# A diffusion block on one core: the order of the first stage (context, conditioning, context keys and values, latent transposes)

## The chip, the cores and the metric

The kernel runs on one core of a Trainium2 chip. The metric is the device time of one execution in microseconds (us), as the median of several runs. The engines of the core are TensorE (PE, matmuls; PEld its weight loads), VectorE (DVE), ScalarE (ACT), GpSimd (POOL) and SyncE (SP, which issues most DMAs). Each engine works through its own list of instructions strictly in the order of that list; an instruction that waits holds back everything behind it on that engine.

## The reference, cut to what matters

```
mod   = split(silu(c)     @ w_ada + b_ada, 6)        # latents: sh1, sc1, g1, sh2, sc2, g2
mod_c = split(silu(c_ctx) @ w_ada + b_ada, 6)        # context: sh1c, sc1c, ...
h_lat = rmsnorm(x,   norm1_g) * (1 + sc1)  + sh1     # 1024 tokens x 1024
h_ctx = rmsnorm(ctx, norm1_g) * (1 + sc1c) + sh1c    #  256 tokens x 1024
# of the context only the keys, the values and the two gate inputs are needed:
k_c, v_c, af_c, ab_c = h_ctx @ w_in[:, ...]          # 512, 1024, 16, 16 columns
q, k, v, r, u, v', af, ab, ga, gb = h_lat @ w_in     # all of them
# two gated linear attention scans (forward, backward) that start from the context's
# state, a gated MLP over chunks, their merge, a residual, a SwiGLU block, a final rmsnorm
```

All is float32. A product is made of three passes over operands that are split into a high part (rounded to the matmul's format) and a low part (the remainder): high x high, high x low, low x high.

## The kernel before, in words

Everything stands in one function, `block_kernel`. The Python code states operations; a scheduler then gives each engine its list, mostly in the order of the code where the code doesn't fix it. `tc.issue_after(i)` fixes that one instruction stands behind another, and `load_in_order` (L245) chains loads on SP this way.

**First stage** (L105 to L403, and the latents' gate inputs at L452):

- *Setup* (L105 to L163): small parameter rows are loaded (`prow`, on ACT's queue), `b_ada` as two rows (`brow`, POOL's queue), the 32 gate columns of `w_in` (`gab`, L137, POOL's queue), the gate weights `wg` (L142, POOL). silu of the two conditioning vectors gives `cs4` (high and low part, 4 columns).
- *Conditioning* (L312 to L331): the first two sixths of `w_ada` (shift, then scale; 1024 columns each) come as sixteen 128x1024 tiles of 512 KB. The loop takes for each of the 8 row blocks k the shift tile and then the scale tile. Each tile is split by ACT (cast, L236) and DVE (subtraction, L237) and then multiplied by PE into four PSUM banks `pada` (L323), which were preset with `b_ada` by eight one-row products (L312). In between DVE lays the gate columns into `graw` (L328, six strided copies), which is split like a weight into `gws` (L331).
- *Context* (L343 on): the two ctx tiles are loaded behind `w_ada` and normalised by `rms_scaled` (L175): ACT squares and sums (L179), DVE scales the sum (L171), POOL raises it to the power -1/2 (L172), DVE multiplies (L181).
- *Columns* (L346 to L361): the four banks are copied to rows (L351), transposed on PE (L353), and give `sh1` and `s1`, the shift and the scale per feature, 8 columns of 128 each.
- *Context operand*: PE transposes the ctx tiles (L190); ACT makes the modulated high part (L194), DVE the exact value (L195), and DVE or POOL their difference (L196, odd k on POOL). These are the 8 high and 8 low slices `hc`.
- *Context products* (L377 to L400): gate inputs (24 products of 256 columns, `mm_fm`, L273), then for each of 4 heads the keys (24, L273) and the values (48, L285, two weight tiles). Every weight tile (512 KB) is loaded into one of 3 `wraw` buffers, split into 2 of the 4 `wspl` buffers (ACT L236, DVE L237), and a `wspl` pair is free again once its 24 products are done. The copies out of PSUM are on ACT (L388, L395). Behind the first value block all eight x tiles are loaded and normalised head by head.
- *Latent operand* (L402, L403): 8 groups of 4 transposes for each half of the tokens, each followed by ACT, DVE and POOL as above; the gate inputs of the latents are 2 x 24 products of 512 columns (L452 to L456).

Then come, per head, gates (`log_gates`, L406; its first product is L413), value, key and query products, and the scans; later stages follow. Tiles of 4 KB per partition come from a pool of 40 `slot` buffers.

## Time and profile before

| | us |
|---|---|
| runs of the kernel before | 1767.29, 1767.95, 1770.74; median 1767.95 |
| the profiled execution, its own time | 1771.97 |
| its span, first to last instruction | 1770.2 (1.8 us lie around it) |
| PE / PEld / DVE / ACT / POOL busy | 1712.4 / 1407.5 / 1138.8 / 668.5 / 215.4 |
| mean granted TensorE clock | 0.993 of 2.4 GHz |

The profile comes from one execution. A page groups instructions by source line, engine and tile; the chain of waits is followed back from the last instruction to what released it. Busy time of PE is modelled, since products overlap in the array; so the spacing of products in a long run is the better price of one. DMA-issuing instructions count as waits of the queue that issues them, not as busy time.

### The profile page before, as it was taken

Reading aid. Unit: us, or ns where it says so; the run is one execution under the profiler, and the core shown is the slowest. Engines: PE = TensorE matmul, PEld = TensorE weight load, DVE = VectorE, ACT = ScalarE, POOL = GpSimd, SP = SyncE. Lnnn points to the kernel's source line nnn. Section 1 sums busy time; section 2 is a strip of 40 time slices with the busy share of each in tenths; the row PEclk is TensorE's granted clock in tenths of the full one; section 3 lists DMA queues with packets and bytes.
Section 4 is the critical chain, followed back from the end, with each engine's and each line's share of the span. In section 5 each row is a group of like instructions: output and inputs, shape, how many; then the busy total and the mean of one; then the engine's idle time right before and its main releaser. Section 6 shows DMA issues by size and latency. Waiting matters only on the chain.

```text
span 1770.2 us, 21603 instructions
## 1 busy us (share of the span) xinstructions
PE 1712.4 (97%) x8162; PEld 1407.5 (80%) x8162; DVE 1138.8 (64%) x1559; ACT 668.5 (38%) x974; POOL 215.4 (12%) x193
## 2 busy tenths in 40 slices
PE   8899999999899999999999999989999999999997
PEld 3887888888678888877888888768888888888886
DVE  7686595867865464277656745885545555466797
ACT  6663423323443434234322213533333333355343
POOL 2220000000112353000000000012122122000001
PEclk9999999999999999999999999989999999999999
DMA  9511234052354454387858951233222232377572
GB/s 339 156 37 36 85 118 179 24 179 60 113 155 133 129 179 125 124 293 260 262 190 308 321 191 74 70 116 98 77 90 83 75 92 84 127 242 277 180 270 99
DMA packets 219961, 267.89 MB, mean 151 GB/s; under 512 B 11920, under 2 KB 142032, under 8 KB 219856
## 3 DMA queue, kind: packets, MB, share of 16 engines
q1 hardware_dynamic: 219040, 265.08, 45.1%
q0 software_dynamic: 720, 1.40, 0.2%
q8 instruction: 64, 1.05, 0.2%
q14 instruction: 41, 0.34, 0.1%
q10 hardware_dynamic: 96, 0.02, 0.0%
HBM read 205.64 MB, written 60.82 MB: 151 GB/s over the span
## 4 chain that ended last, share of the span: by engine, by line
PE 79%; DVE 11%; DMA 4%; issue 3%; ACT 3%; POOL 1%; SPq 0%; DVEq 0%; ACTq 0%; POOLq 0%
PE m L716 20%; PE g L716 17%; PE m L273 13%; PE m L1283 5%; PE g L1283 5%; PE m L1166 5%; PE m L285 4%; PE g L538 2%; DVE s L638 1%; PE m L822 1%; DVE wlo L237 1%; DVE s L422 1%; PE g L822 1%; DMA s<-in_w_ada_dram 1%; PE g L1363 1%
## 5 line engine op out<-in xcount | busy, mean ns | idle before, releaser
L716 PE MATMUL m<-s,s 128*128 128x512 f32 x1320 | 313.5, 395 | 8.8 <-ACT q L736 3.8
L716 PEld LDWEIGHTS m<-s,s 128*128 128x128 f32 x1320 | 251.0, 191 | 65.1 <-ACT q L736 5.8
L273 PE MATMUL m<-s,whi 128*128 128x512 f32 (+1 forms) x832 | 252.3, 384 | 2.2 <-ACT s L990 1.5
L237 DVE TENSOR_TENSOR wlo<-wr,whi 128x1024 fp32r<-128x1024 f32 x92 | 112.4, 1224 | 194.2 <-ACT whi L236 194.0
L716 PE MATMUL g<-s,s 128*128 128x512 f32 x960 | 225.0, 391 | 9.0 <-ACT q L736 4.1
L716 PEld LDWEIGHTS g<-s,s 128*128 128x128 f32 x960 | 179.2, 188 | 51.6 <-ACT q L736 6.6
L273 PEld LDWEIGHTS m<-s,whi 128*128 128x128 f32 x832 | 154.0, 188 | 33.2 <-ACT s L990 2.4
L236 ACT CAST whi<-wr 128x1024 fp32r<-128x1024 f32 x92 | 96.5, 1051 | 214.1 <-PE m L273 107.9
L273 PE MATMUL m<-s,wlo 128*128 128x512 f32 (+1 forms) x416 | 158.9, 383 | 1.8 <-DVE wlo L237 1.8
L637 ACT CAST s<-s 128x1024 fp32r<-128x1024 f32 x98 | 102.4, 1052 | 134.4 <-DVE s L638 62.2
L638 DVE TENSOR_TENSOR s<-s,s 128x1024 fp32r<-128x1024 f32 x98 | 145.4, 1494 | 9.9 <-ACT s L637 6.0
L172 POOL TENSOR_TENSOR rstd<-rstd,nhalf 128x1 f32<-128x1 f32 (+2 forms) x43 | 29.1, 678 | 847.7 <-DVE rstd L171 847.6
L285 PE MATMUL m<-whi,s 128*128 128x256 f32 x640 | 126.0, 291 | 0.1
L716 PE MATMUL g<-s,whi 128*128 128x512 f32 x384 | 118.5, 390 | 0.0
L638 DVE TENSOR_TENSOR s<-wr,s 128x1024 fp32r<-128x1024 f32 x77 | 92.3, 1233 | 22.8 <-ACT s L637 22.1
L285 PEld LDWEIGHTS m<-whi,s 128*128 128x128 f32 x640 | 101.5, 192 | 4.2 <-issue 2.7
L742 POOL TENSOR_TENSOR q<-u,q 128x512 f32<-128x512 f32 x38 | 59.4, 1563 | 314.1 <-DVE u L741 150.3
L637 ACT CAST s<-wr 128x1024 fp32r<-128x1024 f32 x77 | 78.2, 1053 | 49.9 <-DMA wr<-wsT 25.3
L285 PE MATMUL m<-wlo,s 128*128 128x256 f32 x320 | 92.3, 289 | 2.6 <-DVE wlo L237 1.9
L273 PEld LDWEIGHTS m<-s,wlo 128*128 128x128 f32 x416 | 78.3, 188 | 16.6 <-DVE wlo L237 2.0
L1166 PE MATMUL m<-s,s 128*128 128x512 f32 x384 | 87.6, 390 | 0.0
L1166 PEld LDWEIGHTS m<-s,s 128*128 128x128 f32 x384 | 72.0, 188 | 14.9
(293 smaller groups left out, 2879.2 us busy)
## 6 DMA issues: line engine op xcount, KB each, us to landing
wr<-in_w_in_dram SPq DMA_DIRECT2D x82, 512.0 KB
s<-in_w_ada_dram SPq DMA_DIRECT2D x48, 512.0 KB
wr<-in_w_ffn_in_dram SPq DMA_DIRECT2D x48, 512.0 KB
wr<-actd SPq DMA_DIRECT2D x77, 256.0 KB
s<-in_w_ffn_out_dram SPq DMA_DIRECT2D x22, 512.0 KB
wsT<-s SPq DMA_DIRECT2D x44, 256.0 KB
wr<-wsT SPq DMA_DIRECT2D x44, 256.0 KB
wr<-in_w_ffn_out_dram SPq DMA_DIRECT2D x33, 256.0 KB
```

Of the source, the lines that this page charges most:

```text
L236: nc.scalar.copy(hi, raw)
L237: lo_sub[0] = nc.vector.tensor_sub(lo, raw, f(hi)).ins
L273: nc.tensor.matmul(ps, ws[a][:, k, :], get(b, k, t0, n), start=k == 0 and i == 0, stop=k == nk - 1 and i == 2)
L285: nc.tensor.matmul(ps[:, j, :], get(b, 4 * kh + k, (2 * tp + j) * P, P), ws[a][:, k, :], start=kh == 0 and j == 0 and k == 0 and i == 0, s ...
L538: r = nc.tensor.matmul(pkv[:, j, :], kt[:, j, :], vt(n), start=j == 0, stop=True, skip_group_check=True)
L637: nc.scalar.copy(hi, raw)
L638: nc.vector.tensor_sub(lo, raw, f(hi))
L716: pe(nc.tensor.matmul(ps, wts[a][:, k, :], mov[k // 2][b][:, k % 2, :], start=start and k == 0 and i == 0, stop=k == 3 and i == 2, skip_gr ...
L742: nc.gpsimd.tensor_sub(q7, u3, q7)
L822: pe(nc.tensor.matmul(banks[tt], op[mov][kp][b][:, kk, tt * P:(tt + 1) * P], wts[a][:, kk, :], start=start and kp == 0 and kk == 0 and i = ...
L1166: pe(nc.tensor.matmul(ps, yF.get(b, k, tt * P, P), wo[k // 2][a][:, k % 2, :], start=k == 0 and i == 0, stop=k == KT - 1 and i == 2))
L1283: pe(nc.tensor.matmul(banks[tt], o[b][:, 0, tt * P:(tt + 1) * P], o[a][:, 1, :], start=start and k == 0 and i == 0, stop=k == KH - 1 and i ...
```

## The change

It touches the first stage only. The ctx tiles are loaded first and are normalised ahead of everything, their last multiplication on ACT. `w_ada` comes as eight shift tiles, then eight scale tiles (`ada_rows`); the shift columns are made while the scale tiles run. The preset of the banks is gone: `b_ada` comes with the parameter rows and is added to the columns. The gate columns' six copies and their split are moved from DVE and ACT to POOL. All eight ctx transposes stand ahead of the modulation. Gate inputs and first key block of the context are one interleaved group; then come the other three key blocks, and then the eight value blocks, whose weights are loaded in turns with the x tiles; the latents' transposes stand after value blocks 4, 6 and 7, and between the two halves of their gate inputs. Within the stage PE's list is pinned to the order of the code (`mm`, `pe`). Cut to its core:

```diff
-    prow = cst.tile([48, P], F32, name="prow")
-    vecs = [..., (b_alpha_f[0], 4), (b_alpha_b[0], 4)]
+    prow = cst.tile([64, P], F32, name="prow")
+    vecs = [..., (b_alpha_f[0], 4), (b_alpha_b[0], 4), (b_ada[0, 0:2048], 16)]
...
-    brow = [slot([1, 1024]) for _ in range(2)]
-    for n2 in range(2):
-        nc.gpsimd.dma_start(brow[n2], b_ada[0:1, n2 * 1024:(n2 + 1) * 1024])
...
+    def mm(ins):
+        return pe(ins) if pinned[0] else ins
...
-            nc.vector.tensor_scalar(dst, xt, r[:, 0:1], None, op0=ALU.mult)
+            nc.scalar.activation(dst, xt, AF.Copy, scale=r[:, 0:1])
...
-    for k in range(KT):
-        for n2 in range(2):
+    def ada_rows(n2):
+        for k in range(KT):
             w = slot([P, 1024])
             load_in_order(w, w_ada[k * P:(k + 1) * P, n2 * 1024:(n2 + 1) * 1024])
             ws = split_w(w, [P, 1024], pool=True)
...
+    xc = [rms_scaled(t, None, nc.scalar) for t in xc]
+    graw = raw_w([P, KT, P])
+    nc.vector.memset(graw, 0.0)
...
+                nc.gpsimd.tensor_copy(graw[:, :, 64 * d + 16 * q:64 * d + 16 * q + 16], gab[:, :, 16 * d:16 * d + 16])
+        gws = [slot([P, KT, P], F32R) for _ in range(2)]
+        nc.gpsimd.tensor_copy(gws[0], graw)
+        nc.gpsimd.tensor_sub(gws[1], graw, f(gws[0]))
...
+    for _ in ada_rows(0):
+        pass
+    for k, _ in enumerate(ada_rows(1)):
+        if k == 3:
+            columns(0, sh1, bsh)
+        if k >= 5:
+            ctx_T(k - 5)
+    columns(1, s1, bsc)
+    nc.vector.tensor_mul(s1, s1, n1c.unsqueeze(2).to_broadcast([P, 8, 2]))
...
+    kws = split_k(0)
...
+    ctx_products((pa[:, :TC], gws), (pk[:, :TC], kws))
+    aft_evac(aftc, pa[:, :TC])
+    nc.scalar.copy(kc[:, 0, :], pk[:, :TC])
+    for h in range(1, HEADS):
+        kws = split_k(h)
+        pk = bank()
+        ctx_products((pk[:, :TC], kws))
+        nc.scalar.copy(kc[:, h, :], pk[:, :TC])
...
+    ahead = [value_weights(i) for i in range(2)]
+    for i in range(2 * HEADS):
+        ws = ahead.pop(0)
...
+        if i % 2 == 1:
+            for j in range(2):
+                nc.scalar.copy(vc[j][:, i // 2, :], ps[:, j, :])
+        xt = slot([P, D])
+        load_in_order(xt, x[i * P:(i + 1) * P, :])
+        xl.append(rms_scaled(xt))
+        if i + 2 < 2 * HEADS:
+            ahead.append(value_weights(i + 2))
+        if i in (4, 6, 7):
+            lat_groups(*{4: (0, 0), 6: (0, 4), 7: (4, 0)}[i])
```

The lists show where this moves instructions. **POOL, from the load of the gate columns (L137 before, L131 now) on.** `wr` is `graw`, `s` are slot buffers, `rstd` the power of `rms_scaled`. Before, POOL did its setup and then the two powers:

```order
L137 DMA s_112<-in_w_in_dram 128x8x32
...
L148 CAST s_122<-s_123 128x512
L150 MEMSET s_127 128x1024
L172 TENSOR_TENSOR rstd_333<-rstd_333,nhalf 128x1
L172 TENSOR_TENSOR rstd_340<-rstd_340,nhalf 128x1
```

Now:

```order
L131 DMA s_106<-in_w_in_dram 128x8x32
...
L359 COPY wr_165<-s_106 128x8x16
L142 CAST s_116<-s_117 128x512
L144 MEMSET s_121 128x1024
L359 COPY wr_165<-s_106 128x8x16 x5
L187 TENSOR_TENSOR rstd_154<-rstd_154,nhalf 128x1
L361 CAST s_173<-wr_165 128x1024
L362 TENSOR_TENSOR s_174<-wr_165,s_173 128x1024
L187 TENSOR_TENSOR rstd_161<-rstd_161,nhalf 128x1
```

The six copies of the gate columns, which read what L131 loads, now stand ahead of the first power, and the gate weights' cast and subtraction ahead of the second.

**ACT, from the second table load on.** Before, the sixteen casts of `w_ada` tiles followed at once:

```order
L159 ACT_TABLE_LOAD
L236 CAST s_155<-s_153 128x1024
L236 CAST s_165<-s_163 128x1024
```

Now:

```order
L168 ACT_TABLE_LOAD
L194 ACTIVATE s_151,ss_152<-s_147 128x1024
L197 ACTIVATE s_151<-s_147,rstd_154 128x1024
L194 ACTIVATE s_158,ss_159<-s_149 128x1024
L377 CAST s_182<-s_108 128x512
L197 ACTIVATE s_158<-s_149,rstd_161 128x1024
L248 CAST s_189<-s_187 128x1024
L248 CAST s_199<-s_197 128x1024
```

All `w_ada` casts now stand behind two multiplications that need `rstd_154` and `rstd_161`, POOL's two powers.

**ACT again, now, around the second key block and around the last x tile** (`m_438` and `m_439` are the banks of the interleaved group, `m_897` that of the last two value blocks, `s_995` the last normalised x tile):

```order
L365 CAST s_437<-m_438 128x256
L426 COPY s_436<-m_439 128x256
L248 CAST whi_494<-s_492 128x1024
...
L461 COPY s_588<-m_897 128x256
L461 COPY s_589<-m_897 128x256
L194 ACTIVATE s_995,ss_996<-s_993 128x1024
```

The cast of the second key block's weights stands behind the copies of the group before it, and the square of the last x tile behind the copies of the last value block. Behind value block 7, PE's list has the transposes of the second token half, which read `s_995`.

## Rows read from the trace of the kernel before

**Rows 1.** The page, part 1: busy us, share of the span, instructions.

```profile
PE 1712.4 (97%) x8162; PEld 1407.5 (80%) x8162; DVE 1138.8 (64%) x1559; ACT 668.5 (38%) x974; POOL 215.4 (12%) x193
```

**Rows 2.** Windows: stretch, length, busy us per engine (count), PE clock, DMA share, GB/s.

```profile
0.00:37.39 37.39, 29.35 (x97) 8.76 (x98) 27.42 (x50) 25.29 (x29) 9.81 (x24) 0.96 0.92 326
37.39:49.97 12.58, 12.06 (x83) 11.16 (x81) 11.47 (x19) 6.34 (x13) 3.13 (x4) 0.85 0.97 354
49.97:69.57 19.60, 14.59 (x113) 13.50 (x113) 13.92 (x24) 15.31 (x27) 5.49 (x9) 1.00 0.37 104
49.97:105.51 55.54, 49.53 (x359) 45.26 (x359) 39.76 (x54) 34.35 (x56) 18.77 (x16) 1.00 0.41 114
```

**Rows 3.** The chain of waits, first 220 us: start, us, what (products).

```profile
82.48 5.76 PE m L285 x48
88.24 1.75 PE g L190 x16
99.60 4.10 PE m L273 x18
```

**Rows 4.** Timeline, first 48 us: start, us, engine, line, operation, count.

```profile
3.37 0.95 POOL L137 DMA_DIRECT2D s<-in_w_in_dram  x1
8.31 0.61 POOL L148 CAST s<-s 128x512 fp32r<-128x512 f32 x1
8.68 2.94 ACT L236 CAST s<-s 128x1024 fp32r<-128x1024 f32 x3
8.86 0.95 POOL L150 MEMSET s<- 128x1024 f32 x1
26.23 4.62 DVE L237 TENSOR_TENSOR s<-s,s 128x1024 fp32r<-128x1024 f32 x4
31.08 0.18 ACT L179 ACTIVATION_READ_ACCUMULATOR s<-s 128x1 f32 x1
37.14 0.25 DVE L361 TENSOR_TENSOR s<-s,pcol 128x8 f32<-128x8 f32 x2
```

**Rows 5.** The view of line L137, the load of the gate columns.

```profile
DMA to landing us min/median/max: 7.8/7.8/7.8
```

**Rows 6.** Groups by shape, first 107 us: count | busy us, mean ns | idle before.

```profile
L323 PE MATMUL m<-s,cs 128*4 128x512 f32 x64 | 18.4, 421 | 2.6 <-DVE s L237 2.4
L236 ACT CAST s<-s 128x1024 fp32r<-128x1024 f32 x16 | 16.6, 1049 | 4.0 <-DMA s<-in_w_ada_dram 3.9
L196 POOL TENSOR_TENSOR s<-raw,s 128x512 fp32r<-128x512 f32 x8 | 14.4, 1798 | 24.8 <-DVE raw L195 21.2 <-issue 3.6
L179 ACT ACTIVATE s<-s 128x1024 f32<-128x1024 f32 x10 | 10.5, 1058 | 0.0
L181 DVE TENSOR_SCALAR s<-s,rstd 128x1024 f32<-128x1024 f32 x10 | 7.5, 753 | 6.9 <-POOL rstd L172 6.9
L172 POOL TENSOR_TENSOR rstd<-rstd,nhalf 128x1 f32<-128x1 f32 x10 | 5.5, 551 | 37.2 <-DVE rstd L171 37.2
L351 DVE COPY s<-m 4x512 f32<-4x512 f32 x2 | 1.3, 670 | 0.0
L118 POOL DMA_DIRECT2D s<-in_b_ada_dram x2 | 1.2, 585 | 0.3 <-issue 0.3
L372 DVE TENSOR_TENSOR s<-s,s 128x512 f32<-128x512 f32 x1 | 1.1, 1061 | 0.0
L328 DVE COPY wr<-s 128x128 f32<-128x128 f32 x6 | 0.9, 218 | 0.0
```

**Rows 7.** Windows of 2 us around the start of the context products, columns as in rows 2.

```profile
32.00:34.00 2.00, 0.41 (x4) 0.32 (x4) 1.31 (x4) 2.00 (x5) 0.57 (x1) 1.00 0.86 221
38.00:40.00 2.00, 2.00 (x11) 1.92 (x9) 2.00 (x3) 0.61 (x2) 0.00 (x0) 0.50 1.03 408
```

**Rows 8.** Timeline: the last context modulation, and the first gate product.

```profile
46.92 0.91 POOL L196 TENSOR_TENSOR s<-raw,s 128x256 fp32r<-128x256 f32 x1 [1.42 <-DVE raw L195]
105.51 0.50 PE L413 MATMUL g<-s,s 64*128 64x512 f32 x1
```

More of the change, by code (lines that the diff above doesn't have):

```diff
@@ L213, in get @@
             return self.t[part][k // 2][h][:, k % 2, o:o + n]
-    def normed(xs, fm_get, scale, shift):
-        for t0 in range(0, len(xs), 4):
-            grp = xs[t0:t0 + 4]
-            w = P * len(grp)
-            each = 512 // w
-            for k in range(0, KT, each):
-                modulate_T(grp, range(k, k + each), lambda part, k: fm_get(part, k, t0 * P, w), scale, shift, lambda k: k % 2 == 1)
     hc = [[slot([P, 4, TC], F32R) for _ in range(2)] for _ in range(2)]
@@ new lines, in block_kernel, with split_k, ctx_products @@
+    for _ in ada_rows(0):
[7 more added lines that the diff above has]
+    nc.vector.tensor_mul(s1, s1, n1c.unsqueeze(2).to_broadcast([P, 8, 2]))
+    def split_k(h):
+        with tc.issue_after(done[0]), tc.issue_after(done[1]):
+            return split_w(raw_ctx(C_K + h * P), [P, KT, P])
+    def ctx_products(*todo):
+        for k in range(KT):
+            for ps, ws in todo:
+                for i, (a, b) in enumerate(PASS):
+                    mm(nc.tensor.matmul(ps, ws[a][:, k, :], hc_get(b, k, 0, TC), start=k == 0 and i == 0, stop=k == KT - 1 and i == 2))
@@ L406, in log_gates @@
+    aft = slot([P, T], F32R)
+    for h in range(2):
+        ps = bank()
+        mm_fm(ps, gws, hT.get, h * 512, 512)
+        aft_evac(aft[:, h * 512:(h + 1) * 512], ps)
+        if h == 0:
+            lat_groups(4, 4)
+    pinned[0] = False
     def log_gates(d, pieces):
@@ L450, in seq @@
         return slice(n * P, (n + 1) * P)
-    aft = slot([P, T], F32R)
-    for h in range(2):
-        ps = bank()
-        mm_fm(ps, gws, hT.get, h * 512, 512)
-        aft_evac(aft[:, h * 512:(h + 1) * 512], ps)
     def proj(name, n=8):
```

168 lines of the change are left out of this document (85 added, 83 removed).

## The prediction, on record before the change was run

> **What bounds the kernel now.** I read the page's busy shares first [rows 1]: PE is busy for 97% of the span, and no other engine above two thirds. Time can then be won or lost only where PE waits, and the windows show that the first stage has such places [rows 2]: 8.0 us without PE up to 37.39, and 6.0 (55.54 less 49.53) between 49.97 and the first gate product. The chain of waits gives the prices of PE's work in closed runs [rows 3]: 5.76/48 = 0.12 us for a product of 256 columns, 1.75/16 = 0.11 for a transpose, 4.10/18 = 0.23 for a product of 512 columns. The timeline then shows what feeds PE [rows 4]: ACT's casts of `w_ada` begin at 8.68, the scale columns `s1` are ready at 37.39, the last context modulation ends at 46.92 + 0.91 = 47.83 and the first gate product of the latents starts at 105.51 [rows 8].
>
> The change touches only what stands ahead of that product. From there on each engine's list is the same before and after. With PE at 97%, and the later loads issued as buffers come free, a shift of the 105.51 passes to the end at nearly its full size. So the whole sum is one question: when do the latents' gate inputs end now?
>
> **A. The start, on POOL and ACT.** The lists show that all `w_ada` casts stand behind two ACT multiplications, each behind one of POOL's powers, and that the first power stands behind the six copies of gate columns, the second behind their split. So I walk POOL's list.
> - Two loads of `b_ada` leave it, 2 x 0.585 = 1.2 [rows 6]. The issue of the gate columns comes at 3.37 - 1.2 = 2.2 [rows 4]. It took 7.8 to land [rows 5], so 10.0.
> - The six copies: no row has them on POOL; on DVE one takes 0.218 [rows 6]. I take 0.3 each, 1.8. With the cast 0.6 and memset 0.95 that stand among them [rows 4]: 13.3. The bounds for the six are DVE's 1.3 and, at the 0.61 of a whole POOL cast each, 3.7.
> - First power 0.55 [rows 6]: 13.9. ACT multiplication 1.05 (as its square, 1058 ns [rows 6]): 14.9. Second square 1.05 with the read of its sum 0.18 [rows 4]: 16.2.
> - POOL meanwhile casts the gate weights, 1024 columns at twice the 0.61 of 512 [rows 4]: 15.1. Then it subtracts, at twice 1.8 [rows 6]: 18.7. Second power 19.2, multiplication 1.05: **the first `w_ada` cast at about 20.3**, 11.6 later than now.
>
> By the Trainium skill, "GPSIMD Engine Reference", section "3. Performance versus the Vector engine", POOL needs about twice DVE's time on such a subtraction. From the 1.155 that DVE takes [rows 4] that is an estimate of 2.3 instead of 3.6, and by it the first cast would come 1.3 earlier. I keep the 1798 ns of this kernel's own POOL subtractions [rows 6].
>
> **B. From there to the columns.** Before, ACT waited 4.0 for tiles [rows 6]: loads set the pace. Now the tiles lie there, and the slower of ACT (1.05) and DVE (4.62/4 = 1.155 [rows 4]) sets it. 20.3 + 1.05 + 16 x 1.155 = 39.9. DVE also has the shift columns among these splits and waits there for PE: three products' groups, four banks' transposes and two additions, some 2.2 (a bank copy alone is 0.67 [rows 6]): 42.1. The scale columns behind the last split take 2.9 more: **`s1` at 45.0 instead of 37.39, +7.6.** The 11.6 have shrunk by 4 since context squares, splits and rows no longer stand between the last `w_ada` split (26.23 + 4.62 = 30.85) and `s1` [rows 4]. The eight preset products are gone as well; they stood in time that PE had free, and I cost them at nothing.
>
> **C. The context's first products.** Before, the modulations ended 10.4 after `s1`. Now two key splits and the 1.06 subtraction of L372 [rows 6] no longer stand in them, and I take 8. But the first key block's cast is now seventh on ACT behind six modulations (4.5), then cast 1.05 and subtraction 1.2: its low part comes at `s1` + 6.3 = 51.3. 43 products wait behind that: 5.2 at 0.12. The clock adds to it. At 32 to 34, PE was busy for 0.41 of 2 us, and at 38 to 40 its granted clock was 0.50, the 1.2 GHz level [rows 7]. PE now has nothing but sparse products for longer, and I expect the same: 30 products at 0.21 instead of 0.12, +2.7. So gate inputs and first key block end at 51.3 + 5.2 + 2.7 = **59.2, with 48 of 312 context products done.** Before, 246 were left at 49.97 (359 in the window, less 64 transposes, 48 latent products and the gate product [rows 2]): 66 done.
>
> **D. The rest.** PE work: 264 x 0.12 + 64 x 0.11 + 48 x 0.23 = 31.7 + 7.0 + 11.0 = 49.7. Before it was 246 x 0.12 + 18.0 = 47.5, so of the 55.54 [rows 2], 8.0 were waits. PE's list is now pinned, so where it waits, nothing slips in. Walking ACT's and DVE's lists with the prices above:
> - second key block: copy of the bank 0.4, cast 1.05, subtraction 1.15, one behind another: 2.6;
> - fourth value block, whose split stands behind copies, a square and an `rstd` multiplication (0.75 [rows 6]): 1.75;
> - first latent transposes: 0.35;
> - eighth value block: POOL's power stands behind two subtractions of 1.8, and DVE's multiplication ahead of the split: 2.5;
> - the second token half: the last x tile's square stands on ACT behind the copies of the last value block. From there square 1.05 + 0.18, DVE, power 0.55, multiplication 0.75 and the handoffs make 2.8; with the copies and DVE's queue 5.3;
> - the last modulations: 0.85.
>
> Together 13.35 instead of 8.0. 59.2 + 49.7 + 13.35 = **122.2, against 105.51: +16.7**, and half a microsecond for gate products of the first head that slipped in before: about **+17**.
>
> Weight and x loads I cost at nothing: SP issues them as `wraw` buffers come free, and DMA was busy for 0.41 of 49.97 to 105.51 [rows 2], so they have room. If that cover fails, each 512 KB tile adds up to 1.28 (a cast's pitch while loads set it).
>
> The profiled execution took 1771.97, 4 above the median of 1767.95. From it: 1789; from the median, as the result will be given: **1785**.
>
> **Rivals.**
> - *Loads, not POOL, set the start, and PE no longer waits in the blocks: faster.* If the first `w_ada` cast comes by 13 (gate columns landed by 5, POOL's split twice as fast), loads pace the tiles, and two context tiles put ahead cost 2.6: `s1` at about 36 to 37. Then 48 products at 45 and 49.7 of work with 8 of waits make 102.7, and without waits 94.7: 1757 to 1765. It decides at a first cast by 13 and under 8 of waits. Against it: the 7.8 of [rows 5] and ACT's list. Chance 0.09.
> - *The start costs its 7, and the even feeding of x and weights gives it back: no change.* Against it: the last x tile's chain stands in front of PE with 2.8 at least. Chance 0.06; 1764.5 to 1771.5.
> - *The load of the gate columns doesn't hold POOL: less slow.* It shares its time with few others then, and lands before POOL reaches the copies. POOL's own list then puts the first cast at 16.9 (-3.4), PE idles less and the clock may hold (-2.7), and some waits shrink (-2): +9, 1777. By the Trainium skill, "DMA: Bandwidth & Descriptors", section "Anatomy of one DMA — SWDGE (gpsimd) path", a load costs 2.0 us plus its bytes over 436e3 per us, an estimate of 2.3 for these 128 KB; the 7.8 of [rows 5] disagree. For it: the other loads that ran beside it in that profile. Chance 0.22.
> - *More waits than walked: slower still.* PE's clock falls again in the wait for the last x tile, and the subtractions on POOL and DVE hold each other up: +23, 1791. Chance 0.13.
> - *The change doesn't do what it says:* the lists show each move, so I give it nothing.
>
> **How the numbers follow.** The forecast of 1785 has 0.50. The range reaches down to the third rival (1777, less a term's error) and up to the fourth: 1773 to 1793. It takes in the bounds of the copies (-0.5, +1.9) and of the POOL subtraction (-1.3), and leaves out the two rivals on the other side. A measurement of this kernel can tell about 0.2% (3.5 us) from no change. Faster 0.09, same 0.06, slower 0.85.
>
> **What the new profile would show.** The first `w_ada` cast on ACT near 20 (A), no idle between casts but for DVE; the last `s1` operation near 45 (B); granted clock 0.50 as the context products begin, and the interleaved group's end near 59 (C); PE idle of 2.6 at the second key block, and of some 5 ahead of the second half's transposes, released by DVE's last `rstd` multiplication (D); the first gate product near 122. The forecast is wrong if the first cast comes by 13, if PE's waits between 59 and 122 are under 8, or if the later stages take up the shift.

## The result and the profile after

| | before | after the change |
|---|---|---|
| median of the runs, us | 1767.29 | 1785.99 |
| lowest to highest | 1766.97 to 1770.74 | 1782.56 to 1786.80 |
| ratio, 95% interval | | 1.0099 [1.0084, 1.0113] |
| span of the profiled execution | 1770.2 | 1785.1 |

The changed kernel is slower by 18.7 us, 1%. The page shows the same work in a longer span: PE has 8 products fewer (the preset) and is busy for 5 us less than in [rows 1], although some of its products ran at the lower clock.

```profile
PE 1707.0 (96%) x8154; PEld 1410.9 (79%) x8154; DVE 1134.1 (64%) x1548; ACT 668.5 (37%) x975; POOL 216.9 (12%) x199
```

**The start.** Timeline of the changed kernel, first 41 us, as in [rows 4], with two rows of SP's queue. L175 is the transpose of the parameter rows, L359 are the gate columns' copies, L187 the first power, L362 the gate columns' subtraction (what stands above as the gate weights' cast and subtraction on POOL is theirs too; the gate weights `wg` are split on ACT and DVE), L248 and L249 the casts and subtractions of `w_ada`, L343 a column bank's copy, L402 the last operation on `s1`.

```profile
6.88 0.30 POOL L359 COPY wr<-s 128x128 f32<-128x128 f32 x1
8.57 1.22 POOL L359 COPY wr<-s 128x128 f32<-128x128 f32 x5
8.67 0.34 PE L175 MATMUL g<-ident,prow 64*128 64x64 f32 x1 [5.66 <-DMA prow<-in_b_ada_dram]
10.44 0.57 POOL L187 TENSOR_TENSOR rstd<-rstd,nhalf 128x1 f32<-128x1 f32 x1 [0.65 <-DVE rstd L186]
12.08 2.34 POOL L362 TENSOR_TENSOR s<-wr,s 128x1024 fp32r<-128x1024 f32 x1
16.62 11.46 ACT L248 CAST s<-s 128x1024 fp32r<-128x1024 f32 x12
17.68 13.71 DVE L249 TENSOR_TENSOR s<-s,s 128x1024 fp32r<-128x1024 f32 x12 [1.40 <-ACT s L248]
31.31 0.67 DVE L343 COPY s<-m 4x512 f32<-4x512 f32 x1
33.40 4.62 DVE L249 TENSOR_TENSOR s<-s,s 128x1024 fp32r<-128x1024 f32 x4
36.58 0.61 SPq L263 DMA_DIRECT2D s<-in_x_dram  x1
41.01 0.17 DVE L402 TENSOR_TENSOR s<-s,pcol 128x16 f32<-128x16 f32 x1
67.69 0.37 SPq L263 DMA_DIRECT2D wr<-in_w_in_dram  x1
```

The first cast of `w_ada` stands at 16.62, forecast 20.3. The copies began at 6.88, when POOL was done with its DMA issues, and took 0.24 each; POOL's power then waited for DVE. DVE came to the sum at 10.20, though ACT had it ready at 8.72: its list has the copy of the parameter columns ahead of it, which waited for PE's transpose of the rows, and that for the load of `b_ada`, which the change has put into these rows. The load of the gate columns landed 4.6 us after its issue at 1.83, so it held nobody; it was 7.8 in [rows 5]. View of the line of that load:

```profile
DMA to landing us min/median/max: 4.6/4.6/4.6
```

From the first cast on, DVE's sixteen splits set the pace, with the shift columns (31.31 to 33.40) between them. `s1` is complete at 41.18: 3.8 later than before, not 7.6.

**The groups by shape**, first 121 us, columns as in [rows 6]: ACT's casts of `w_ada` waited for nothing (before: 4.0 us for tiles), and its one wait for a tile is 0.9 us for the first ctx tile. From the first cast to the gate products, no load sets any pace.

```profile
L248 ACT CAST s<-s 128x1024 fp32r<-128x1024 f32 x16 | 15.3, 1041 | 0.0
...
L194 ACT ACTIVATE s<-s 128x1024 f32<-128x1024 f32 x10 | 10.6, 1064 | 0.9 <-DMA s<-in_ctx_dram 0.9
```

**The windows**, columns as in [rows 2]:

```profile
0.00:41.18 41.18, 21.50 (x95) 8.76 (x96) 26.18 (x41) 24.11 (x29) 14.13 (x30) 1.00 0.97 327
41.18:54.76 13.58, 9.47 (x52) 8.35 (x52) 7.43 (x14) 5.44 (x10) 2.92 (x4) 0.75 0.23 80
...
54.76:120.18 65.42, 56.07 (x371) 52.10 (x371) 41.02 (x57) 36.36 (x59) 15.77 (x16) 0.90 0.41 129
...
46.00:48.00 2.00, 0.92 (x4) 0.62 (x4) 2.00 (x4) 0.28 (x1) 0.04 (x1) 0.50 0.00 0
...
60.00:62.00 2.00, 2.00 (x11) 2.00 (x11) 0.00 (x0) 0.00 (x0) 0.00 (x0) 0.52 0.00 0
...
96.00:98.00 2.00, 1.98 (x9) 1.99 (x10) 1.27 (x3) 0.00 (x0) 0.55 (x1) 0.51 0.37 73
...
106.00:108.00 2.00, 2.00 (x9) 1.81 (x8) 1.88 (x3) 2.00 (x4) 0.00 (x0) 0.50 0.80 215
...
148.00:150.00 2.00, 2.00 (x7) 1.54 (x7) 0.00 (x0) 0.07 (x1) 0.00 (x0) 0.50 0.00 0
```

54.76 is the end of the interleaved group, 120.18 the first gate product of the latents. In that last stretch the granted clock is 0.90 on average; the three 2-us windows of it that are shown tell why: behind PE's waits the clock stands near 0.50, the 1.2 GHz level. Before, it was 1.00 throughout that stretch [rows 2].

**PE's waits**, timeline of PE (L413 the context's gate inputs and key products, L455 value products, L208 transposes, L282 the latents' gate inputs, L486 the first gate product, L515 the first transposes of the scan):

```profile
45.64 0.79 PE L413 MATMUL m<-s,whi 128*128 128x256 f32 x2 [2.20 <-ACT whi L248]
47.51 0.58 PE L413 MATMUL m<-s,wlo 128*128 128x256 f32 x1 [1.08 <-DVE wlo L249]
...
56.52 0.50 PE L413 MATMUL m<-s,whi 128*128 128x256 f32 x2 [1.77 <-ACT whi L248]
57.78 0.39 PE L413 MATMUL m<-s,wlo 128*128 128x256 f32 x1 [0.76 <-DVE wlo L249]
...
78.20 0.39 PE L455 MATMUL m<-wlo,s 128*128 128x256 f32 x1 [1.30 <-DVE rstd L186]
...
96.02 0.58 PE L455 MATMUL m<-wlo,s 128*128 128x256 f32 x1 [2.04 <-DVE rstd L186]
...
104.06 3.03 PE L208 MATMUL g<-ident,s 128*128 128x128 f32 x13 [3.32 <-DVE s L199]
...
120.18 0.49 PE L486 MATMUL g<-s,s 64*128 64x512 f32 x1
120.95 1.32 PE L282 MATMUL m<-s,s 128*128 128x512 f32 x5
...
147.09 0.58 PE L515 MATMUL g<-ident,s 128*128 128x128 f32 x2 [1.82 <-DVE s L1011]
```

The two releases "DVE rstd L186" are tiny operations that the profile names because they end last; what PE's product reads is the low half `wlo`, DVE's subtraction just ahead of them (94.75 + 1.22 = 95.97 for the second). With one wait of 0.18 at 84.3, the waits in five places between 54.76 and 120.18 make 9.35 us. The longest one, 3.32, is the end of this chain (view: the chain of waits; POOL L217 is a modulation's low part, L187 the power, L199 the last x tile's multiplication):

```profile
101.06 1.32 POOL s L217
102.39 0.08 issue
102.48 0.19 issue
102.67 0.56 POOL rstd L187
103.23 0.03 issue
103.25 0.77 DVE s L199
```

**Where the stage ends.** Before, all 48 gate-input products of the latents stood ahead of the first gate product. Now the first gate product has slipped in ahead of the last five of them (the rows of 120.18 and 120.95 above), so its time no longer marks their end. The gate inputs themselves end at 122.10, where the next product starts, against 105.51 before: +16.6. That is 3.8 at `s1` and 12.8 from there on: 80.92 us instead of 68.12, of which PE waits for 13.5 instead of 6.5 and is busy for 67.45 instead of 61.59, at a mean clock of 0.87 instead of 0.97.

**Behind the stage** the order is the same but for such slips around the first gates, and the shift of the same product against before was +16.3 at the scan's first transposes (130.8 before, 147.09 now), +17.7 some 10 us later, and +19.2 at 1014.8 us of before. From there to the end it falls to +14.8, because the profiled execution of *before* lost about 4.5 at 1150 to 1166 (granted clock 0.50 to 0.60 in most of it) and this one didn't. So I take the product at 1014.8 as the landmark below; its +19.2 agrees with the 18.7 of the medians.

### The profile page after: what moved, and what is told of

The parts are those of the page before. It is cut to its first block, busy times and chain, and to the rows that moved or that the text cites. A ratio compares the mean times of both kernels' runs of the same rounds, so it can differ in the third digit from the quotient of the medians.

```text
span 1785.1 us, 21573 instructions
## 1 busy us (share of the span) xinstructions
PE 1707.0 (96%) x8154; PEld 1410.9 (79%) x8154; DVE 1134.1 (64%) x1548; ACT 668.5 (37%) x975; POOL 216.9 (12%) x199
## 3 DMA queue, kind: packets, MB, share of 16 engines
q8 instruction: 64, 1.05, 0.2%
## 4 chain that ended last, share of the span: by engine, by line
PE 77%; DVE 11%; ACT 3%; DMA 3%; issue 2%; POOL 1%; SPq 0%; DVEq 0%; POOLq 0%; ACTq 0%
PE m L774 18%; PE g L774 17%; PE m L282 13%; PE m L1341 5%; PE g L1341 5%; PE m L1224 5%; PE m L294 3%; DVE s L696 2%; PE g L605 1%; PE m L880 1%; DVE s L495 1%; PE g L880 1%; PE g L1421 1%; DMA s<-vd 1%; DVE wlo L249 1%
## 5 line engine op out<-in xcount | busy, mean ns | idle before, releaser
L774 PE MATMUL m<-s,s 128*128 128x512 f32 x1320 | 308.5, 390 | 9.5 <-ACT q L794 3.8
L282 PE MATMUL m<-s,whi 128*128 128x512 f32 x768 | 239.1, 392 | 2.0 <-ACT s L1048 1.4
L249 DVE TENSOR_TENSOR wlo<-wr,whi 128x1024 fp32r<-128x1024 f32 x88 | 107.5, 1224 | 191.8 <-ACT whi L248 191.3
L248 ACT CAST whi<-wr 128x1024 fp32r<-128x1024 f32 x88 | 92.2, 1050 | 207.3 <-PE m L282 104.9
L282 PEld LDWEIGHTS m<-s,whi 128*128 128x128 f32 x768 | 143.3, 188 | 32.9 <-ACT s L1048 2.3
L282 PE MATMUL m<-s,wlo 128*128 128x512 f32 x384 | 149.7, 391 | 0.0
L187 POOL TENSOR_TENSOR rstd<-rstd,nhalf 128x1 f32<-128x1 f32 (+2 forms) x43 | 29.7, 692 | 848.9 <-DVE rstd L186 848.9
L294 PE MATMUL m<-whi,s 128*128 128x256 f32 x512 | 102.9, 294 | 0.0
L1224 PE MATMUL m<-s,s 128*128 128x512 f32 x384 | 87.6, 390 | 0.0
L294 PEld LDWEIGHTS m<-whi,s 128*128 128x128 f32 x512 | 81.8, 192 | 4.0 <-issue 2.9
L282 PEld LDWEIGHTS m<-s,wlo 128*128 128x128 f32 x384 | 72.2, 188 | 14.7
L774 PEld LDWEIGHTS g<-s,whi 128*128 128x128 f32 x384 | 72.0, 188 | 14.8
L1224 PEld LDWEIGHTS m<-s,s 128*128 128x128 f32 x384 | 72.0, 188 | 14.8
```

Source lines behind the costliest of these rows:

```text
L187: nc.gpsimd.tensor_tensor(r[:, :n], r[:, :n], nhalf[:, :n], op=ALU.pow)
L248: nc.scalar.copy(hi, raw)
L249: nc.vector.tensor_sub(lo, raw, f(hi))
L282: mm(nc.tensor.matmul(ps, ws[a][:, k, :], get(b, k, t0, n), start=k == 0 and i == 0, stop=k == nk - 1 and i == 2))
L294: mm(nc.tensor.matmul(ps[:, j, :], get(b, 4 * kh + k, (2 * tp + j) * P, P), ws[a][:, k, :], start=kh == 0 and j == 0 and k == 0 and i == 0 ...
L774: pe(nc.tensor.matmul(ps, wts[a][:, k, :], mov[k // 2][b][:, k % 2, :], start=start and k == 0 and i == 0, stop=k == 3 and i == 2, skip_gr ...
```

## The experiments

My theory was that two things make the time: PE's waits for operands that ACT, DVE and POOL finish late, and the lower clock behind them. The rivals: the late start (the first cast at 16.62) carries the loss; or pinning PE's list does; or PE's waits are filled at no gain, as they are only passed on. Eleven kernels tell these apart, each timed 4 to 11 times beside the kernel before on the same chip. "To before" is the distance of its median to the median of the kernel before beside it; "landmark" is the profiled execution's shift at the product named above; `s1` is the end of the columns, gate the first gate product, and inputs the end of the latents' gate inputs. In e6, c2 and c3, 11 of the 48 gate-input products stand behind the first gate product, in the others 5; so kernels are compared by the inputs.

| kernel | median | ratio to before, 95% | to before | first steady cast | s1 | gate | inputs | landmark |
|---|---|---|---|---|---|---|---|---|
| before | | | | 8.7 | 37.4 | 105.5 | 105.5 | 0 |
| the change | 1785.99 | 1.0099 [1.0084, 1.0113] | +18.7 | 16.6 | 41.2 | 120.2 | 122.1 | +19.2 |
| e1_last_x | 1783.19 | 1.0089 [1.0075, 1.0102] | +15.7 | 16.6 | 42.4 | 117.9 | 119.9 | +13.9 |
| e4_gate_late | 1788.50 | 1.0116 [1.0103, 1.0130] | +21.0 | 15.6 | 44.1 | 122.8 | 124.7 | +21.0 |
| e5_key_pool | 1783.52 | 1.0089 [1.0075, 1.0103] | +16.0 | 16.6 | 46.4 | 119.9 | 121.8 | +15.3 |
| e7_fill | 1781.65 | 1.0080 [1.0067, 1.0093] | +14.2 | 16.6 | 41.0 | 117.0 | 118.9 | +12.7 |
| e8_start | 1784.21 | 1.0092 [1.0078, 1.0106] | +15.4 | 9.9 | 41.9 | 120.1 | 122.0 | +16.4 |
| e9_key_dve | 1781.95 | 1.0080 [1.0067, 1.0092] | +13.1 | 16.5 | 42.4 | 117.5 | 119.4 | +13.8 |
| e10_blocks | 1780.57 | 1.0070 [1.0057, 1.0083] | +11.8 | 16.7 | 41.1 | 116.0 | 117.9 | +11.2 |
| c1 | 1776.34 | 1.0044 [1.0030, 1.0057] | +7.5 | 10.9 | 40.1 | 112.0 | 113.9 | +8.8 |
| e6_unpin | 1784.07 | 1.0090 [1.0075, 1.0105] | +16.0 | 16.6 | 40.9 | 112.5 | 117.6 | +15.3 |
| c2 | 1769.75 | 1.0008 [0.9999, 1.0016] | +1.7 | 10.9 | 37.1 | 102.9 | 106.9 | +1.2 |
| c3 | 1765.77 | 0.9998 [0.9988, 1.0008] | -0.8 | 11.0 | 37.3 | 99.1 | 103.3 | -2.5 |

### The last x tile earlier (e1_last_x)

```diff
-        xt = slot([P, D])
-        load_in_order(xt, x[i * P:(i + 1) * P, :])
-        xl.append(rms_scaled(xt))
+        for t in {6: (6, 7), 7: ()}.get(i, (i,)):
+            xt = slot([P, D])
+            load_in_order(xt, x[t * P:(t + 1) * P, :])
+            xl.append(rms_scaled(xt))
```

> Edit: the last x tile is normalised together with the seventh, ahead of the modulations of the first token half, instead of behind the last value block; nothing else. In the changed kernel PE waits 3.3 us (100.75 to 104.06) for that tile, and its granted clock is 0.50 from 104 to 108. Theory A (the waits of the first stage, each followed by a stretch at the lower clock, are the loss): that wait goes, the clock stays at 1.00 there, and about 5 us are won, 1781. Theory B (ACT and DVE are short of time in the blocks, so that a wait removed comes back at another place): the modulations of the first half are 2 us later, PE waits that much in front of the gate inputs, and the time stays within 1.5 us of 1786.

The wait of 3.32 became two, 0.93 and 1.80, and behind them only the window from 104 to 106 stood at 0.50 (0.77 and 0.88 on its sides). The landmark moved by 5.3, the distance to before by 3.0, with overlapping intervals. The chain of the last x tile is a cost, but PE's next wait, for a bank that a DVE modulation (L216) still reads, is not far behind.

### The start: the gate columns' split out of the way (e4_gate_late), and everything out of the way (e8_start)

In e4 the gate columns' cast and subtraction stand behind the second power on POOL:

```diff
-        nc.gpsimd.tensor_copy(gws[0], graw)
-        nc.gpsimd.tensor_sub(gws[1], graw, f(gws[0]))
+        with tc.issue_after(last_pow[0]):
+            nc.gpsimd.tensor_copy(gws[0], graw)
+            nc.gpsimd.tensor_sub(gws[1], graw, f(gws[0]))
```

> Edit: on POOL the cast and the subtraction of the gate columns stand behind the second power instead of ahead of it. In the changed kernel the second power ends at 15.5, and the w_ada casts begin at 16.62. Theory A (POOL's list sets the start): the second power ends near 14.0, the casts begin near 15.2, DVE's splits at 16.3, behind its work on the gate weights, and s1 comes 1.4 us earlier: 1784.5. Rival (the loads or DVE's own list set the pace of the splits): the casts begin earlier, but s1 stays at 41.2 and the time at 1786.

The first cast came 1.0 earlier, and everything else later. Timeline of e4, DVE and POOL (L381 is the subtraction of the gate weights `wg` in 512 columns, L365 that of the gate columns):

```profile
15.12 2.36 POOL L365 TENSOR_TENSOR s<-wr,s 128x1024 fp32r<-128x1024 f32 x1
...
15.82 2.20 DVE L381 TENSOR_TENSOR s<-s,s 128x512 f32<-128x512 f32 x1 [2.41 <-ACT s L380]
```

L381 took 1.15 in the changed kernel and 2.20 here: it ended at 18.03, 0.55 after POOL's subtraction (17.48), which had begun first. In the changed kernel, too, POOL's had begun first and L381's counterpart ended 0.55 after it (14.97 and 14.42). In e8, where this operation starts ahead of POOL's, it takes 0.68; so the 1.15 already holds a wait for POOL. In e4 DVE's splits then began at 19.25 instead of 17.68 and `s1` came 2.9 later. My theory fell here, and so did the rival: an earlier first cast is worth nothing when the DVE behind it is held.

In e8 the ctx loads come behind the shift tiles, the ctx multiplications are back on DVE, and the split of `wg` stands behind the modulations:

```diff
-    xc = [rms_scaled(t, None, nc.scalar) for t in xc]
...
     for _ in ada_rows(0):
         pass
+    xc.extend(rms_scaled(t) for t in rows_of(ctx_in, NTC))
...
+    with tc.issue_after(done[0]), tc.issue_after(done[1]):
+        wgh = slot([P, 512], F32R)
+        nc.scalar.copy(wgh, wg)
```

> Edit: the ctx tiles are loaded behind the shift tiles instead of first, their multiplications are on DVE instead of ACT, and the preparation of the gate weights (one cast, three DVE operations) stands behind the context's modulations; nothing behind that is changed. Theory A (the late w_ada casts are what makes s1 late): the casts begin near 8 instead of 16.62, the loads set the pace, s1 comes at 36.5 instead of 41.2, and 4 to 5 us are won: 1781. Rival (POOL's subtraction of the gate columns now runs beside DVE's splits and doubles them, as a POOL subtraction did in the run of the key blocks, and PE's products of w_ada fall to the lower clock): s1 at 39 to 40, at most 2 us won.

Casts ran steadily from 9.88, 6.7 earlier, and `s1` was complete at 41.88, no earlier at all. Timeline of e8:

```profile
10.88 11.33 DVE L249 TENSOR_TENSOR s<-s,s 128x1024 fp32r<-128x1024 f32 x8
11.02 3.30 POOL L358 TENSOR_TENSOR s<-wr,s 128x1024 fp32r<-128x1024 f32 x1
22.13 0.14 DVE L186 TENSOR_SCALAR rstd<-ss 128x1 f32<-128x1 f32 x1
...
29.65 0.67 DVE L343 COPY s<-m 4x512 f32<-4x512 f32 x1
32.40 0.17 DVE L346 TENSOR_TENSOR sh<-g,pcol 128x16 f32<-128x16 f32 x1 [2.08 <-PE g L345]
```

DVE's first split came 6.8 earlier, and its list lost that again in four places: eight splits beside POOL's subtraction (11.33 for 8 x 1.155 = 9.24), the ctx chain from 22.13 to the next split at 25.11 (3.0), the shift columns from 29.65 to 32.70 (3.05 instead of 2.1, of which 2.08 are a wait for PE), and the scale columns, 1.4 longer, as PE reached them later. So early casts buy nothing by themselves. That a late start costs nothing isn't shown, though: behind a first cast at 16.62, sixteen splits of 1.155 and the 3.2 of the scale columns can't end before about 39 (an estimate from these rows), and the kernels below that come to 37 have the early casts as well.

### The key blocks prepared early: on POOL (e5_key_pool) and on DVE (e9_key_dve)

Both cast the first two key blocks on ACT before the scale columns. e5 subtracts on POOL; e9 on DVE, the first behind the last `w_ada` split, the second behind the modulations:

```diff
+    def key_early(h):
+        raw = raw_ctx(C_K + h * P)
...
+        early[0] = nc.scalar.copy(hi, raw).ins
+        nc.gpsimd.tensor_sub(lo, raw, f(hi))
...
-    columns(1, s1, bsc)
+    ks = [key_early(h) for h in range(2)]
+    with tc.issue_after(early[0]):
+        columns(1, s1, bsc)
```

> Edit: the first two key blocks of the context are split before the scale columns, their casts on ACT where it sat idle for 6 us, their subtractions on POOL, instead of behind the modulations on ACT and DVE. Theory A: the waits of 2.2 and 1.1 us inside the first context products and of 1.8 and 0.8 us in front of the second key block go, the clock comes back to 1.00 sooner and does not fall again at 58 us: 6 to 8 us less, 1778 to 1780. Theory B: the modulations (8 x 0.95 us on DVE) hold PE just as long, and the third key block or the first value weights become late: at most 2 us less.

The waits went: from `s1` to the gate product 73.5 us instead of 79.0. But `s1` came 5.2 later. Timeline of e5, the last four splits on DVE beside the two subtractions on POOL:

```profile
33.24 8.97 DVE L249 TENSOR_TENSOR s<-s,s 128x1024 fp32r<-128x1024 f32 x4
34.09 5.91 POOL L399 TENSOR_TENSOR wlo<-s,whi 128x1024 fp32r<-128x1024 f32 x2 [18.55 <-ACT whi L398]
```

The same four splits took 4.62 in the changed kernel, and POOL's subtraction alone takes 2.34. One after another that makes 4.62 + 2 x 2.34 = 9.30, and the two engines together needed 8.97. Operation by operation they took turns: from 34.46 on the ends are DVE's, POOL's (36.69), DVE's (37.77), POOL's (39.99) and DVE's (41.08), 2.2 us for each of POOL's and 1.1 for each of DVE's. By the Trainium skill, "SBUF — State Buffer", section "Who interferes with whom", a DVE instruction with two inputs in SBUF and a GpSimd instruction that reads SBUF contend for a shared port, which one of them holds for a whole instruction while the other is blocked. These numbers agree with it, and so does e4, where the later starter ended 0.55 after the earlier one's end, less than its own 0.68.

```diff
+        if h == 0:
+            sub0[0] = nc.vector.tensor_sub(lo, raw, f(hi)).ins
...
+    with tc.issue_after(done[0]), tc.issue_after(done[1]):
+        nc.vector.tensor_sub(ks[1][1], ks[1][2], f(ks[1][0]))
```

> Edit: the first two key blocks are cast ahead of the scale columns, in ACT's idle time, the first one's subtraction is on DVE behind the last w_ada split, the second one's behind the modulations; nothing of it is on POOL. Theory A: s1 stays where it was (41 to 42.4, as the clock falls in the last w_ada products or not), the waits of 2.2, 1.1, 1.8 and 0.8 us go, and with the clock 5 to 6 us are won: 1780.5. Rival (the subtraction stands ahead of the copy of the scale row on DVE and makes s1 late by its 1.2 us, and the modulations pace PE anyway): at most 2 us.

On DVE the same idea works: `s1` only 1.2 later, the 2.20 and 1.08 among the modulations gone but for 0.55, the gate product 2.7 earlier, 5.6 us less in the median's distance (the intervals still overlap). The wait of the second key block was handed to the third (1.41 and 0.76, from 55.3 and 57.2).

### The clock by itself (e7_fill)

30 transposes of the identity stand ahead of the transposes of the second token half; nothing reads their results.

```diff
-    def modulate_T(xn_tiles, ks, dst, scale, shift, flip):
+    def modulate_T(xn_tiles, ks, dst, scale, shift, flip, fill=0):
...
         pt = gbank()
+        for _ in range(fill):
+            mm(nc.tensor.transpose(pt[:, :P], ident, ident))
```

> Edit: 30 further transposes of the identity matrix, whose results nobody reads, stand on PE ahead of the transposes of the second token half, where PE waits for 3.3 us; they take 30 x 0.11 = 3.3 us at full clock. The wait itself stays. Theory A with the clock as a loss of its own: the granted clock stays at 1.00 from 104 on, the 16 transposes and the products behind them run at full speed, and 2 to 2.8 us are won, 1783.5. Rival (ACT's and DVE's modulations pace PE there anyway, the lower clock costs nothing): the clock stays up, and the time stays at 1786 or grows by up to 0.5.

More work on PE, and less time: 4.5 us less in the distance to before (the intervals still overlap), 6.5 at the landmark. Timeline of e7, PE:

```profile
98.25 3.44 PE L207 MATMUL g<-ident 128*128 128x128 f32 x30
101.52 0.49 PE L210 MATMUL g<-ident,s 128*128 128x128 f32 x3
103.55 1.64 PE L210 MATMUL g<-ident,s 128*128 128x128 f32 x13 [1.54 <-DVE s L199]
```

The fill lies in the wait for the last x tile, of which 1.54 is left. The 13 transposes took 1.64 instead of 3.03, and from their start to the gate product it was 13.4 us instead of 16.1. PE waits in neither stretch and the products are the same, so those 2.7 are the clock's. Windows of e7 (the changed kernel had 0.50 from 104 to 108):

```profile
104.00:106.00 2.00, 2.00 (x16) 1.83 (x15) 1.90 (x3) 2.00 (x3) 0.00 (x0) 1.00 0.07 18
```

That the fill kept the clock up is borne out by the other profiles: eight of them have an unfilled wait of 3.27 to 4.81 at these transposes (the changed kernel, e4, e5, e8, e9, e10, c1, c2), and in each the clock stood near 0.50 in the 4 us behind it. The rest of the gain isn't the fill's: in this execution the clock also stayed at 1.00 behind the wait at 93.5 (2.05), where it fell to 0.51 in the changed kernel's profile (2.04). Behind waits of about 2 us falls come and go: behind this one the clock fell in two of the seven profiles that have it (the changed kernel and e9) and stayed at 1.00 in e1, e4, e5, e7 and e8. That may be part of why a profile and a median differ by 1 to 2 us.

### The value blocks in another order (e10_blocks)

The next weights are split first, then the x tile's normalisation, then the copies out of PSUM; the last two x tiles come in one turn; the last copies stand behind the modulations.

```diff
-        if i % 2 == 1:
-            for j in range(2):
-                nc.scalar.copy(vc[j][:, i // 2, :], ps[:, j, :])
...
         if i + 2 < 2 * HEADS:
             ahead.append(value_weights(i + 2))
+        for t in {6: (6, 7), 7: ()}.get(i, (i,)):
...
+                if i == 7:
+                    with tc.issue_after(lat_mod[0]):
+                        nc.scalar.copy(vc[j][:, i // 2, :], ps[:, j, :])
```

> Edit: in the turns of value blocks and x tiles the split of the weights two blocks ahead stands first, then the x tile's normalisation, then the copies of the block; the last x tile is normalised with the seventh, ahead of the modulations, and the copies of the last block stand behind these. Theory A: the waits of 1.3, 2.05 and 3.3 us between value block 4 and the second token half go, the clock doesn't fall at 96 and at 102, and 8 to 9 us are won: 1777. Theory B (ACT and DVE are full in this stretch, a wait comes back in front of the gate inputs): 3 us at most.

The waits at the fourth and the eighth value block are gone (one of 1.13 is new, from 82.0), 6.9 us less in the distance. But waits of 3.27 and 1.21 have taken the place of 3.32. Timeline of e10, PE and DVE:

```profile
96.87 0.75 DVE L199 TENSOR_SCALAR s<-s,rstd 128x1024 f32<-128x1024 f32 x1 [0.73 <-POOL rstd L187]
97.54 1.52 DVE L216 TENSOR_SCALAR raw<-g,s,sh 128x512 f32<-128x512 f32 x2
98.40 1.97 PE L208 MATMUL g<-ident,s 128*128 128x128 f32 x8 [3.27 <-DVE raw L216]
```

Now PE waits for a bank that DVE reads (L216), and L216 stands behind the normalisations of x tiles, each behind a power on POOL. It is the same DVE queue with another instruction at its head.

### The three together (c1)

```diff
+    xc.extend(rms_scaled(t) for t in rows_of(ctx_in, NTC))
...
+    ks = [key_early(h) for h in range(2)]
...
+        for t in {6: (6, 7), 7: ()}.get(i, (i,)):
```

> The three edits of the runs named start, key blocks on DVE, and blocks, together. If they add up: 4.5 + 5.5 + 8.5 = 18.5 us less than the changed kernel, 1767.5, the time of the kernel before, with the first gate product at 102 to 103. If the same waits are only handed on (each edit uncovers the next late work): 1773 to 1777.

11.2 us less than the change. Alone, e8, e9 and e10 gave 3.3, 5.6 and 6.9, together 15.8, so about seven tenths add up. The 3.27 and 1.21 stayed, and DVE was busy in 16.43 of the 20 us from 84 to 104.

### PE's list not pinned (e6_unpin)

```diff
     def mm(ins):
-        return pe(ins) if pinned[0] else ins
+        return ins
```

> Edit: PE's list in the first stage is no longer pinned to the order of the code; the scheduler places its products as in the kernel before. Everything else as in the changed kernel. If the pinned list is what turns late operands into waits (nothing slips in where PE waits): the gaps of 2.2 to 3.3 us shrink to half or less, 4 to 6 us won, 1780 to 1782. If the operands themselves are late, made by ACT, DVE and POOL in the same order as now: within 2 us of 1786.

PE's waits between `s1` and its first gate product fell from 13.5 to 6.5 us, as little as in the kernel before, because other products slip in: the gaps shrank as the first branch said, but the time by 2.7 us only, with overlapping intervals. Some of it came back later: at the scan's first transposes PE waits for 3.44 us instead of 1.82, with the clock at 0.50 behind it. So the pin costs little: the operands are late, and products that are pulled ahead into a gap leave PE waiting for the next late ones.

### DVE's list relieved (c2), and the x tiles fed ahead (c3)

c2 is c1 with five moves: the gate columns' subtraction on DVE ahead of the first `w_ada` split; the ctx multiplications behind later splits; the shift columns' additions behind the last split; the third key block's cast ahead of the copy; the next stage's first splits behind the second half's modulations.

```diff
-        nc.gpsimd.tensor_sub(gws[1], graw, f(gws[0]))
+        nc.vector.tensor_sub(gws[1], graw, f(gws[0]))
...
+                with tc.issue_after(sub[0]):
+                    nc.vector.tensor_scalar(dst, t, r[:, 0:1], None, op0=ALU.mult)
...
-            columns(0, sh1, bsh)
+            pc0 = columns(0, sh1, bsh)
...
+        columns_add(pc0, sh1, bsh)
...
+            ks.append(split_k(2))
...
+    hold.extend(held)
```

> The combination c1, in which s1 came at 40.1 and the first gate product at 112.0, with what its trace shows to be left: the subtraction of the gate columns is on DVE ahead of the first w_ada split, not on POOL beside them (beside them 8 splits took 11.3 us instead of 9.3); the two ctx multiplications stand behind two more splits, so that DVE doesn't wait for POOL's powers (3.0 us with the waits); the additions of the shift columns stand behind the last split, so that DVE doesn't wait for PE (1.6 us); the third key block's cast stands ahead of the copy of the second (waits of 1.4 and 0.8); the next stage's weight splits stand behind the modulations of the second token half (2.4 us of DVE). If these waits were what held s1 and the blocks: s1 at 36.5 to 37.5, the first gate product at 103 to 106, 1766 to 1770. If DVE's sheer work in the blocks (busy throughout from 85 to 105 in c1) sets the end: s1 at 37, but the first gate product not before 108, 1772.

`s1` at 37.09, as before the change, and 17.0 of the 18.7 us are back. With the start of the casts as in c1 (10.9), `s1` came 3.0 earlier by these moves. Left were a wait of 1.13 for an x tile and the 3.27 of e10, with clock 0.50 behind it.

c3 is c2 with the x tiles loaded three ahead (in the changed kernel SP issued nothing from 36.58 to 67.69, as the next value weights waited for a `wraw` buffer and the x tiles stood behind them), squared one block ahead, and multiplied behind the weight's subtraction:

```diff
+    for t in range(3):
+        x_load(t)
+    x_square(0)
+    x_mult(0)
...
+        if i + 1 < 2 * HEADS:
+            x_square(i + 1)
...
+        if i + 1 < 2 * HEADS:
+            with tc.issue_after(sub[0]):
+                x_mult(i + 1)
+        x_load(i + 3)
```

> The combination c2, in which s1 came at 37.1 and the first gate product at 102.9 (105.5 in the kernel before), but where PE still waited 1.1 us at 71 and 3.3 us at 84 and its clock stood at 0.50 from 88 to 94. There DVE's list had three chains of scaling, power on POOL and multiplication behind each other (81.2 to 86.8, of which 3.1 us waiting for POOL) ahead of the modulations. Edit: x tiles are loaded three ahead and squared one block ahead of their turn, the power runs beside the weight split, and the multiplication stands behind it. If these chains were the last wait: no gap over 1 us behind 60 us, no fall of the clock there, the first gate product at 97 to 99, 1763 to 1766. If DVE's sheer work is the limit: the gap moves in front of the gate inputs, 1768 to 1770.

It is 19.5 us better than the change, and within the measurement's error of the kernel before (0.9998 [0.9988, 1.0008]). Against c2 the gain of 2.5 lies inside the intervals. PE's waits from `s1` to the gate product are 3.5 us, and the window from 84 to 104 has PE busy for 19.14 of 20 us at clock 1.00. DVE is busy there for 17.38 us, more than in c1, so its sheer work wasn't the limit. The first gate product stands at 99.1, 6.4 earlier than before the change, but 11 of the gate-input products stand behind it; they end at 103.3, 2.2 earlier than before, and at the scan's first transposes 2.6 are left. Windows and timeline of c3:

```profile
84.00:104.00 20.00, 19.14 (x111) 15.82 (x111) 17.38 (x24) 10.04 (x16) 12.43 (x7) 1.00 0.28 79
```

```profile
128.19 0.44 PE L592 MATMUL g<-ident,s 128*128 128x128 f32 x2 [1.76 <-DVE s L1088]
```

From the end of the gate inputs to these transposes it takes 24.9 us, before 25.3 (in all kernels here 24.9 to 25.4). No kernel here is measurably faster than the one before.

## Why the prediction was right, and where it wasn't

The time (1785.99 for 1785, slower) was right. But that the sum met it to within 1 us is luck: errors of 3.7 and 4.0 on one side and 8.3 on the other cancel in it.

| step | forecast | measured | error |
|---|---|---|---|
| A, first `w_ada` cast | 20.3 | 16.62 | -3.7 |
| B, from there to `s1` | 24.7 | 24.56 | -0.1 |
| C, from `s1` to the end of the interleaved group | 14.2 | 13.58 | -0.6 |
| D, PE's work | 49.7 | 57.99 | +8.3 |
| D, waits | 13.35 | 9.35 | -4.0 |
| end of the latents' gate inputs | 122.2 | 122.10 | -0.1 |
| shift from there to the landmark | +0.5 | +2.6 | +2.1 |

- **A failed in its first term.** That the load of the gate columns holds POOL until 10.0 was wrong: the load landed at 1.83 + 4.6 = 6.4 and POOL came to the copies at 6.88, later than it. The rival that said so gave 16.9 for the first cast, and 16.62 came. Its time (1777) was wrong all the same, because it let PE's waits and the clock shrink along with it. The estimate of 2.3 us for that load, by the Trainium skill's DMA page named there, isn't borne out either: 4.6 now, 7.8 before. The subtraction was 2.34 us, not the 3.6 that I took from POOL's rows in the context stage: this one ran while DVE was nearly idle. The Trainium skill's estimate of 2.3 ("GPSIMD Engine Reference", section "3. Performance versus the Vector engine") was the better price, but only without DVE; in e8, beside DVE, the same operation took 3.30. As B was right, A's error passed into `s1` at full size (41.18 for 45.0).
- **B was right**, for the reason given: DVE's 1.155 per split and the shift columns among them. c2 bears it out from the other side: with early casts and DVE's list relieved, `s1` came back to 37.1.
- **C was right** in size and mechanism: the first key block's split among the modulations holds PE (2.20 + 1.08), and the clock falls to 0.50. The low part came 6.28 after `s1`, forecast 6.3; but the terms written there (4.5, 1.05 and 1.2) make 6.75. The six modulations took 3.4 on ACT instead of 4.5, and DVE came to the subtraction 0.7 after the cast. e9 took most of this wait away.
- **D's waits all stood where the walk put them**, each at or under its size: 2.53 for 2.6 (second key block), 1.30 for 1.75 (fourth value block), 0.18 for 0.35 (first latent transposes), 2.04 for 2.5 (eighth value block), 3.32 for 5.3 (last x tile), none for 0.85 (modulations). The 9.35 they make stand against 6.0 before by the same measure, busy time [rows 2]; the prediction's 8.0 for before came from a lower price of PE's work.
- **The clock behind the waits was missing from D.** I had priced it at the start and left it to a rival here. From 54.76 to 122.10 PE is busy for 57.99 us, where the products were priced at 49.7. Seven of its 2-us windows in which PE worked have a low clock (0.63, 0.52, 0.51, 0.63, 0.50, 0.50, 0.57); what they lack of 1.00 makes 2 x 3.14 = 6.3. Of the other 2.0, 0.8 are the first gate product and two value products that slipped in, and the rest is the low price. e7 shows 2.7 of the 6.3 as the clock's own. The other half of that rival, POOL and DVE holding each other up, showed in this kernel only by tenths (the second power, beside a DVE subtraction, took 1.14 instead of 0.55), and at length in e4, e5 and e8.
- **"Passes to the end at nearly its full size" was low.** The 16.6 grew to 17.7 in the first head and to 19.2 at the landmark. The trace shows a longer wait at the scan's start (1.82 for 1.32) with the clock at 0.50 behind it, where before it stayed at 1.00; that fall, too, comes and goes (in e5, e7, e8 and e10 the clock stayed at 1.00 behind the same wait). No run took the growth by itself, so its cause stays open.
- **Loads at nothing** held: no wait of PE, ACT or DVE between 41 us and the end of the gate inputs ends at a load. Only c3 loads the x tiles further ahead, together with the squares, and its gain over c2 is inside the error.

So the 18.7 us are in waits for late operands and in the clock behind them, and most of the new order isn't bound to have them. c2 and c3 keep shift ahead of scale, the interleaved group, keys ahead of values, weights and x in turns, the transposes among the blocks and the pinned list, and cost nothing that can be measured. Some parts of the change they give up: the ctx tiles are loaded behind the shift tiles and not first, their last multiplication is on DVE again, and so is the gate columns' subtraction. What made the change slow was the place of small operations in the lists of DVE, ACT and POOL; whether it could stay with ctx first wasn't tried.

## What to carry to other kernels

When an order of work is changed, walk the list of the engine that feeds the busiest one (here DVE), operation by operation: an earlier start of another engine alone brought `s1` no earlier (e8), while three regroupings of small operations gave back 11.2 of 18.7 us (c1) and five further moves 5.8 (c2). Price a wait of PE together with the lower clock that may stand behind it, from rows of the same kernel at that level; filling such a wait with work that nobody reads may pay (e7, by 4.5 us with overlapping intervals). Compare kernels at the same point of the work: a first product that slips ahead of the rest is no such point. Before work is moved from DVE to POOL, look for what DVE does in that moment.

## What the runs showed of the hardware that I had not expected

- Two-input subtractions on DVE and POOL take turns: 8.97 us for what takes 4.62 and 4.68 alone (e5). A 512-column one of DVE, 0.68 where it starts first (e8), takes 1.15 in the changed kernel and 2.20 in e4, and in both ends 0.55 after POOL's, which had started first. POOL's 1024-column one takes 3.30 instead of 2.34 beside DVE (e8).
- 30 more transposes cost no time and probably won some: behind a filled wait the same stretch took 13.4 us instead of 16.1 (e7).
- Waits of 3.27 to 4.81 us at the second token half's transposes were followed by a clock near 0.50 in all eight profiles that have one. The wait of 2.04 to 2.06 us at the eighth value block was followed by 0.51 in the changed kernel and by 1.00 in e7.
